# A two-layer trunk on one Trainium2 core: four reorderings in the projections and around the convolution output

## The chip, the cores and the metric

The kernel runs on one NeuronCore of a Trainium2 chip. The metric is the device time of one launch in microseconds; the number given for a kernel is the median of several runs. Besides that one execution is recorded by the hardware profiler, and all rows below come from it. The engines are PE (TensorE, matmuls), DVE (VectorE), ACT (ScalarE), POOL (GpSimd) and SP (SyncE, which here only issues DMAs). A DMA is issued by SP's or POOL's queue and runs beside the engines.

## The reference, cut to what matters

The trunk has two layers on a sequence of 1024 tokens with 1024 channels, all float32.

```python
# layer 0: gated short convolution
h = rms_norm(x, conv_norm)
b, c, u, z = split(h @ conv_w_in, 4)             # conv_w_in: 1024 x 8192
v = c * u
y = b * sum(conv_w[k] * shift(v, k)) * silu(z)   # causal, width 3
x1 = x + y @ conv_w_out                          # 2048 x 1024
# layer 1: dilated window attention, 3 groups x 16 heads of 64
h = rms_norm(x1, attn_norm)
qkv, z = split(h @ attn_w_in)                    # 3 groups x (q, k, v), and z
q, k = rms_norm(q, q_gain), rms_norm(k, k_gain)
o_g, lse_g = window_attention(q, k, v, rel_bias[t5_bucket])   # per group g
o = sum(softmax_g(lse_g) * o_g)
out = x1 + (o * silu(z)) @ attn_w_out
```

The row statistics of both norms (one factor per token) are applied after the products, since they commute with them.

## The kernel before

The work lies transposed: channels on the 128 partitions, tokens along the free axis, the tokens in two halves of 512 (`hf` 0 and 1). Every float32 operand of a product is split into a high part (ACT, line 169 for weights) and a low part (DVE, line 170), and a product is three matmuls: high with high, high with low, low with high. All matmuls of the projections are 128x128 with 512 columns.

There are four stages.

1. The convolution projections. 16 blocks `e` of 128 columns, four weights each (u, c, z, b). Blocks 0 and 1 are plain products (`products`, 24 matmuls each, lines 377 to 379). Blocks 2 to 15 go through `strassen`: two weights make a unit of seven products of 12 matmuls each (lines 304 to 307), on sums and differences of the four quadrants (T[1] to T[4] and the blocks B). Two units make one block e: in the first (`pr` = 0) u and c, in the second z and b. The seven products of a unit run in the order 1, 2, 4, 6, 5, 3, 7, where 4 and 3 are those of the unit before. `prepare` loads the two weights of the next unit meanwhile (SP, line 164, two raw tiles in all), forms four sums on POOL (line 279, the "mixes") and splits seven weights (eight "ws" tiles). A bank that more than one product adds to is first copied out by ACT (`copied`, line 312).
2. The convolution output: eight output tiles `dt` for each token half, 48 matmuls each (`chunk`, lines 554 to 556). `row` adds x, stores x1 to DRAM (line 565), and prepares the operands of the attention projections. In the second half it forms V1[i] and T[1] for dt = i under 4, and T[2] for dt = i + 4; both take the x1 of the first half back from DRAM (line 542).
3. The attention projections, again by `strassen`. T[3], T[4] and the lower block are made by `third`, `fourth` and `lower`, which are put between the products of the first two units. The product with T[3] is the last of the first unit.
4. The attention and its output product.

The row statistics of layer 0: `square` sums the squares of the x tiles on ACT and DVE into `sqacc`; `row_stats` takes the column sums by eight small matmuls for a half (line 94) into the one bank of the pool "cst", and DVE computes the reciprocal root in eleven small operations (lines 68 to 72); `row_spread` spreads it by four transposes (line 246) into that same bank, and ACT copies it to R and squares it to R2 (lines 247, 248). The evacuations `evac` of u, c and z need R or R2.

The tables of relative biases: `tables(v)` makes the bias of group v as one row per head (`vecd`, line 262), and `skew(v, h0)` writes it 128 times with a shift per copy, for four heads, into a DRAM table (line 268): a DMA on POOL's queue of 768 KB, or 512 KB for the third group. Twelve of them are traced, one at the start of the first unit of each block e from 4 to 15 (`between`). They are read in stage 4.

The order of the work: on PE the order of the program text holds everywhere. ACT is bound to it in the stretch from the first load to the end of block 0 (`manual_schedule`). Everywhere else, and on DVE, POOL and SP throughout stages 1 to 3, a planner orders the instructions when the kernel is built: it takes what is ready soonest by its own costs, so an instruction without open inputs can move ahead of others in the text. On each queue instructions then run strictly in the planned order. Tiles come from pools of fixed size; "f" has 12 tiles of 128x512, and a load into one waits for its last reader.

Of the kernel before, what the change touches and what calls it, by code (L numbers as in the profile page):

```python
# [19 lines left out]
P = 128  # L20
# [15 lines left out]
def trunk(ctx: ExitStack, tc: tile.TileContext, a, out):  # L36
# [103 lines left out]
    with tc.tile_pool(name="wq", bufs=1) as wq, tc.tile_pool(name="sle", bufs=1) as sle, \  # L140
# [32 lines left out]
        def load_x(hf):  # L173
            for kt in range(KT):
                xt = X[hf, kt] = ftile()
                if kt % 4 == 0:
                    B[kt // 4, hf] = block("abfg"[2 * hf + kt // 4])
                if hf == kt == 0:
                    r0 = raw_w(a["conv_w_in"][0, 0], 2)
                    W[0] = [split_w(r0[:, :HALF])]  # L180
                nc.sync.dma_start(xt, a["x"][hf, kt])
# [4 lines left out]
                if hf == kt == 0:  # L186
                    W[0].append(split_w(r0[:, HALF:]))
# [78 lines left out]
        def skew(v, h0):  # L266
            sk, w = ((sk0, 384), (sk1, 384), (sk2, 256))[v]
            nc.gpsimd.dma_start(sk[h0:h0 + 4].rearrange("h (i m) -> i h m", m=w + 1)[:, :, :w],
                                vecd[v, h0:h0 + 4][None, :, :w].to_broadcast([P, 4, w]))
# [68 lines left out]
        with tc.tile_pool(name="rp", bufs=1, side="right") as rp, tc.tile_pool(name="cp", bufs=2, side="right") as cp, \  # L338
# [62 lines left out]
            with tc.manual_schedule(engines={mybir.EngineType.Activation}):  # L401
# [15 lines left out]
                ps[1, 1] = products(1, 1, pp)  # L417
                row_spread(0)
                row_stats(1)
                ps[2, 1] = products(2, 1, pp)  # L420
                row_spread(1)
# [3 lines left out]
                ps[3, 0] = products(3, 0)  # L425
# [84 lines left out]
        with tc.tile_pool(name="ev", bufs=1, side="right", reuse_waits="tile") as ev, tc.tile_pool(name="xb", bufs=1, side="right", reuse_waits="tile") as xb, \  # L510
# [34 lines left out]
            B, T, V1 = {}, {}, {}  # L545
# [12 lines left out]
            def row(hf, dt):  # L558
# [19 lines left out]
                else:  # L578
# [4 lines left out]
                    parts_of(T[2], i, t)  # L583
                if dt == 0:
# [6 lines left out]
            def next_half(q):  # L591

                if q == 0:
                    load_y(1, 0)
                    for dt in range(2):
                        WO[dt, 0] = out_w(dt, 0)
                else:
                    load_y(1, q)

            load_y(0, 0)  # L600
            for dt in range(2):
# [3 lines left out]
            for hf in range(2):  # L605
                for dt in range(2):
                    WO[dt, 1] = out_w(dt, 1)
                for q in range(4):
                    for dt in range(2):
                        chunk(hf, dt, q)  # L610
                for dt in range(KT):
                    if dt > 1:
                        for c in range(2):
                            WO[dt, c] = out_w(dt, c)
                        if hf == 0 and dt == KT - 1:
                            next_half(0)
                        for q in range(4):
                            chunk(hf, dt, q)
                            if hf == 0 and dt == KT - 1 and q < 3:
                                next_half(q + 1)  # L620
                    row(hf, dt)
                    if hf == 1 and dt == 2:
                        stats(0, cst, sm)
                    elif hf == 1 and dt == 3:
                        spread(0, rtok, cst)
                    elif hf == 1 and dt == 4:
# [159 lines left out]
            def third(i):  # L786
                if i == 0:
                    T[3] = block("g")
                t = x1_tile(0, i)
                nc.vector.scalar_tensor_tensor(t, t, ng2[:, i:i + 1], V1[i], op0=OP.mult, op1=OP.add)  # L790
                parts_of(T[3], i, t)
# [451 lines left out]
```

## Time and profile before

| | |
|---|---|
| median of 3 runs | 2038.78 us (2037.06 to 2042.22) |
| profiled execution | 2040.09 us, its span 2038.1 us |
| PE busy | 1958.5 us, 96% |
| DVE, ACT, POOL busy | 1481.0 (73%), 903.5 (44%), 879.8 us (43%) |
| granted clock of PE, mean | 0.988 |
| moved by DMA | 254.25 MB, mean 125 GB/s |

How to read the rows below: times are in us from the span's start unless marked ns. In a row of the timeline the first number is the start, the second the length, then engine, line, operation, output and inputs; in brackets the idle time of the engine before it and what ended it. A matmul's length includes its way through the array, so the spacing of two starts is its cost. In rows of waits the engine and line that waited stand left of the arrow and what it waited for on the right. A granted clock of 1.00 is 2.4 GHz, 0.50 is 1.2 GHz.

### The profile page before, as it was taken

The numbers are of one execution on the slowest core, as the hardware profiler recorded it, in microseconds if no ns is written. First come the engines' busy times: TensorE is split into PE (matmuls) and PEld (weight loads), VectorE is DVE, ScalarE is ACT, GpSimd is POOL, SyncE is SP. The second block draws the span as 40 slices with busy tenths as digits, with TensorE's granted clock in tenths as the row PEclk, the third lists the DMA queues.
The fourth block names the chain that finished last, engine by engine and source line by source line (L and its number), as shares of the span: only waits on it lengthen the run. The fifth ranks groups of instructions, "written<-read, shape, count | busy, mean of one in ns | idle before, by whom it ended". The sixth has DMA issues, their size and how long they took to land. (4 is left out here: it accounts for less than half of the span.)

```text
span 2038.1 us, 29437 instructions
## 1 busy us (share of the span) xinstructions
PE 1958.5 (96%) x10302; PEld 1585.0 (78%) x10302; DVE 1481.0 (73%) x2751; ACT 903.5 (44%) x2042; POOL 879.8 (43%) x800
## 2 busy tenths in 40 slices
PE   7999999999999999999999999999999988898998
PEld 6887778888888888788888888888888866666666
DVE  6866566566666555798888888788888847767686
ACT  5433233333334344434344343444343358757570
POOL 0356566666665212434455445544445522322220
PEclk9999999999999999999999999999999999999999
DMA  5316512112214564423333233323233368766632
GB/s 189 114 62 146 141 61 73 68 67 73 72 64 152 178 228 159 131 76 111 102 105 123 84 111 97 123 83 121 86 124 104 91 241 248 219 175 207 181 115 84
DMA packets 116805, 254.25 MB, mean 125 GB/s; under 512 B 15822, under 2 KB 22718, under 8 KB 116656
## 3 DMA queue, kind: packets, MB, share of 16 engines
q1 hardware_dynamic: 93024, 177.42, 26.2%
q0 software_dynamic: 23632, 74.95, 12.9%
q8 instruction: 81, 1.33, 0.3%
q14 instruction: 68, 0.56, 0.1%
HBM read 193.05 MB, written 67.64 MB: 128 GB/s over the span
## 5 line engine op out<-in xcount | busy, mean ns | idle before, releaser
L170 DVE TENSOR_TENSOR ws<-wr,ws 128x512 fp32r<-128x512 f32 x284 | 270.2, 953 | 131.8 <-ACT ws L169 130.3
L169 ACT ACTIVATE ws<-wr 128x512 fp32r<-128x512 f32 x284 | 178.4, 630 | 395.6 <-PE pp L307 230.7
L169 ACT ACTIVATE ws<-sr 128x512 fp32r<-128x512 f32 x272 | 169.6, 629 | 295.9 <-PE pp L307 246.6
L279 POOL TENSOR_TENSOR sr<-wr 128x512 f32<-128x512 f32 x136 | 185.2, 1362 | 262.8 <-DMA wr<-in_conv_w_in 66.5
L170 DVE TENSOR_TENSOR ws<-sr,ws 128x512 fp32r<-128x512 f32 x272 | 235.6, 873 | 82.6 <-ACT ws L169 80.9
L898 ACT ACTIVATE xs<-xs,nl 128x128 f32<-128x128 f32 (+1 forms) x384 | 167.9, 439 | 91.2 <-DVE nl L895 80.2
L316 DVE TENSOR_TENSOR f<-pp,f 128x512 f32<-128x512 f32 x204 | 139.5, 684 | 85.5 <-PE pp L307 80.9
L895 DVE CUSTOM_DVE_ANT_0 xs<-ps,bt 128x128 f32<-128x128 f32 (+1 forms) x384 | 110.9, 347 | 79.5 <-PE ps L887 57.8
L312 ACT ACTIVATE f<-pp 128x512 f32<-128x512 f32 x228 | 132.5, 581 | 28.4 <-POOL blkc L683 13.4
L279 POOL TENSOR_TENSOR sr<-wr,sr 128x512 f32<-128x512 f32 x68 | 89.1, 1310 | 81.2 <-issue 57.6
L716 POOL DMA_DIRECT2D qkd<-blkc x96 | 68.1, 716 | 129.2 <-DVE blkc L711 121.8
L674 ACT ACTIVATE f<-f 128x512 f32<-128x512 f32 x96 | 60.7, 633 | 135.8 <-DVE f L316 98.8
L304 PE MATMUL pp<-blke,ws 128*128 128x512 f32 x272 | 108.7, 400 | 8.2 <-ACT f L312 8.2
L304 PE MATMUL pp<-blkg,ws 128*128 128x512 f32 x272 | 107.5, 395 | 4.8 <-ACT f L312 3.8
L306 PE MATMUL pp<-blkg,ws 128*128 128x512 f32 x272 | 106.7, 392 | 3.3 <-DVE blkg L524 3.3
L304 PE MATMUL pp<-blkf,ws 128*128 128x512 f32 x272 | 108.5, 399 | 0.7 <-ACT f L312 0.7
L304 PE MATMUL pp<-blka,ws 128*128 128x512 f32 x272 | 107.3, 395 | 0.7 <-ACT f L312 0.7
L306 PE MATMUL pp<-blke,ws 128*128 128x512 f32 x272 | 107.9, 397 | 0.0
L307 PE MATMUL pp<-blke,ws 128*128 128x512 f32 x272 | 107.8, 396 | 0.0
L304 PE MATMUL pp<-blkb,ws 128*128 128x512 f32 x272 | 107.4, 395 | 0.0
L304 PE MATMUL pp<-blkd,ws 128*128 128x512 f32 x272 | 107.0, 393 | 0.0
L887 PE MATMUL ps<-qk 64*128 64x128 f32 (+1 forms) x768 | 91.4, 355 | 15.7 <-DVE nl L895 8.6
(305 smaller groups left out, 5398.4 us busy)
## 6 DMA issues: line engine op xcount, KB each, us to landing
wr<-in_conv_w_in SPq DMA_DIRECT2D x128, 256.0 KB, 2.9
wr<-in_wqk SPq DMA_DIRECT2D x96, 256.0 KB, 3.0
qkd<-blkc POOLq DMA_DIRECT2D x96, 256.0 KB, 3.2
qk<-qkd SPq DMA_DIRECT2D x48, 512.0 KB, 7.1
wr<-in_conv_w_out SPq DMA_DIRECT2D x64, 256.0 KB, 3.2
f<-in_x SPq DMA_DIRECT2D x48, 256.0 KB, 4.5
wr<-in_wv SPq DMA_DIRECT2D x48, 256.0 KB, 2.9
vd<-f POOLq DMA_DIRECT2D x48, 256.0 KB, 2.4
```

What stands on the lines that cost most here:

```text
L169: nc.scalar.activation(t[:, 0], src, AF.Copy)
L170: nc.vector.tensor_tensor(t[:, 1], src, t[:, 0].bitcast(F32), op=OP.subtract)
L279: nc.gpsimd.tensor_tensor(t, x, y, op=op)
L304: nc.tensor.matmul(ps, w[:, 0, ws], b[:, k, 0], start=new and k == 0, stop=False, skip_group_check=not new)
L306: nc.tensor.matmul(ps, w[:, 0, ws], b[:, k, 1], start=False, stop=False, skip_group_check=not new)
L307: nc.tensor.matmul(ps, w[:, 1, ws], b[:, k, 0], start=False, stop=end and k == 3, skip_group_check=not new)
L312: nc.scalar.activation(t, ps, AF.Copy)
L316: nc.vector.tensor_tensor(m, ps, m, op=OP.add)
L716: nc.gpsimd.dma_start(qkd[hp, g, which].rearrange("p (c s) -> p c s", c=c) [:, :, hf * m:(hf + 1) * m], o.rearrange("p (c s) -> p c s", c=c))
L887: nc.tensor.matmul(out_, q[hs, b * P:(b + 1) * P], k[hs, kv], start=True, stop=True)
L895: nc.vector.tensor_tensor_reduce(out=x, in0=ps[s][:, x0:x0 + nk].rearrange("p a b -> p (a b)"), in1=u["bt"][s][:, bs], op0=OP.add, op1=OP. ...
L898: nc.scalar.activation(x, x, AF.Exp, bias=nm, scale=-1.0, accum_out=L)
```

## The change

Four edits; no arithmetic is added or left out.

1. `load_x`: the load of the first x tile is issued ahead of the two halves of the first weight (they were issued ahead of it). The split of the weight's first half follows the split of x tile 0, and that of its second half follows x tile 1.
2. `skew`: each of the twelve DMAs is bound behind the instruction that stands before it in the program text on POOL (`keep_in_program_order` sets an edge of issue order, without a wait for completion). From block 6 on that instruction is the last mix of the unit before.
3. Block 0: `row_spread(0)` and `row_stats(1)` move behind `products(2, 1)`, and `row_spread(1)` moves behind `products(3, 0)`; that product takes its bank from the pool "pp" and not from "cps".
4. The convolution output takes its tiles as 0, 4, 1, 5, 2, 6, 3, 7. For dt = i + 4 in the second half `row` now also loads the x1 tile i of the first half again and forms V3[i]; `third` only splits V3[i] into its two parts, where it loaded and formed it before. The places of `stats`, `spread` and `next_half` are counted by the position in the new order.

```diff
--- before.py
+++ after.py
@@ -175,15 +175,16 @@
                 xt = X[hf, kt] = ftile()
                 if kt % 4 == 0:
                     B[kt // 4, hf] = block("abfg"[2 * hf + kt // 4])
+                nc.sync.dma_start(xt, a["x"][hf, kt])
                 if hf == kt == 0:
                     r0 = raw_w(a["conv_w_in"][0, 0], 2)
-                    W[0] = [split_w(r0[:, :HALF])]
-                nc.sync.dma_start(xt, a["x"][hf, kt])
                 hi, lo = (B[kt // 4, hf][:, kt % 4, i] for i in range(2))
                 nc.scalar.activation(hi, xt, AF.Copy, scale=g1[:, kt:kt + 1])
                 nc.vector.scalar_tensor_tensor(lo, xt, g1[:, kt:kt + 1], hi.bitcast(F32), op0=OP.mult,
                                                op1=OP.subtract)
                 if hf == kt == 0:
+                    W[0] = [split_w(r0[:, :HALF])]
+                if hf == 0 and kt == 1:
                     W[0].append(split_w(r0[:, HALF:]))
                 if hf == 1:
                     square(0, kt)
@@ -265,8 +266,9 @@
 
         def skew(v, h0):
             sk, w = ((sk0, 384), (sk1, 384), (sk2, 256))[v]
-            nc.gpsimd.dma_start(sk[h0:h0 + 4].rearrange("h (i m) -> i h m", m=w + 1)[:, :, :w],
-                                vecd[v, h0:h0 + 4][None, :, :w].to_broadcast([P, 4, w]))
+            tc.keep_in_program_order(
+                nc.gpsimd.dma_start(sk[h0:h0 + 4].rearrange("h (i m) -> i h m", m=w + 1)[:, :, :w],
+                                    vecd[v, h0:h0 + 4][None, :, :w].to_broadcast([P, 4, w])))
 
         def prepare(s1_, s2_):
 
@@ -415,14 +417,14 @@
                     square(1, kt)
                 plain_w(0, 3, 2)
                 ps[1, 1] = products(1, 1, pp)
+                ps[2, 1] = products(2, 1, pp)
                 row_spread(0)
                 row_stats(1)
-                ps[2, 1] = products(2, 1, pp)
-                row_spread(1)
                 for k in range(3):
                     evac(0, k, 0, ps[k, 0])
                 next(mix)
-                ps[3, 0] = products(3, 0)
+                ps[3, 0] = products(3, 0, pp)
+                row_spread(1)
                 for k in range(3):
                     evac(0, k, 1, ps[k, 1])
                 evac(0, 3, 0, ps[3, 0])
@@ -542,7 +544,7 @@
                 nc.sync.dma_start(t, x1d[kt, :, half(hf)])
                 return t
 
-            B, T, V1 = {}, {}, {}
+            B, T, V1, V3 = {}, {}, {}, {}
             WO, ps = {}, {}
 
             def chunk(hf, dt, q):
@@ -581,6 +583,8 @@
                     t = V1[i]
                     nc.vector.scalar_tensor_tensor(t, x1, g2[:, dt:dt + 1], t, op0=OP.mult, op1=OP.subtract)
                     parts_of(T[2], i, t)
+                    t = V3[i] = x1_tile(0, i)
+                    nc.vector.scalar_tensor_tensor(t, t, ng2[:, i:i + 1], V1[i], op0=OP.mult, op1=OP.add)
                 if dt == 0:
                     nc.scalar.activation(sqacc[:, cs], x1, AF.Square)
                 else:
@@ -592,38 +596,39 @@
 
                 if q == 0:
                     load_y(1, 0)
-                    for dt in range(2):
+                    for dt in order[:2]:
                         WO[dt, 0] = out_w(dt, 0)
                 else:
                     load_y(1, q)
 
+            order = [0, 4, 1, 5, 2, 6, 3, 7]
             load_y(0, 0)
-            for dt in range(2):
+            for dt in order[:2]:
                 WO[dt, 0] = out_w(dt, 0)
             for q in range(1, 4):
                 load_y(0, q)
             for hf in range(2):
-                for dt in range(2):
+                for dt in order[:2]:
                     WO[dt, 1] = out_w(dt, 1)
                 for q in range(4):
-                    for dt in range(2):
+                    for dt in order[:2]:
                         chunk(hf, dt, q)
-                for dt in range(KT):
-                    if dt > 1:
+                for n, dt in enumerate(order):
+                    if n > 1:
                         for c in range(2):
                             WO[dt, c] = out_w(dt, c)
-                        if hf == 0 and dt == KT - 1:
+                        if hf == 0 and n == KT - 1:
                             next_half(0)
                         for q in range(4):
                             chunk(hf, dt, q)
-                            if hf == 0 and dt == KT - 1 and q < 3:
+                            if hf == 0 and n == KT - 1 and q < 3:
                                 next_half(q + 1)
                     row(hf, dt)
-                    if hf == 1 and dt == 2:
+                    if hf == 1 and n == 2:
                         stats(0, cst, sm)
-                    elif hf == 1 and dt == 3:
+                    elif hf == 1 and n == 3:
                         spread(0, rtok, cst)
-                    elif hf == 1 and dt == 4:
+                    elif hf == 1 and n == 4:
                         spread(0, ms2, cst)
 
 
@@ -786,9 +791,7 @@
             def third(i):
                 if i == 0:
                     T[3] = block("g")
-                t = x1_tile(0, i)
-                nc.vector.scalar_tensor_tensor(t, t, ng2[:, i:i + 1], V1[i], op0=OP.mult, op1=OP.add)
-                parts_of(T[3], i, t)
+                parts_of(T[3], i, V3[i])
 
             def fourth(i):
                 if i == 0:
```

## Rows read from the trace of the kernel before

**Rows 1.** Page, part 1: busy time, share of the span, instructions

```profile
PE 1958.5 (96%) x10302; PEld 1585.0 (78%) x10302; DVE 1481.0 (73%) x2751; ACT 903.5 (44%) x2042; POOL 879.8 (43%) x800
```

**Rows 2.** Windows of 100 us: each engine's busy time (matmuls), granted clock, DMA share

```profile
200.00:300.00 100.00, 92.19 (x384) 74.34 (x383) 60.06 (x64) 32.84 (x57) 58.46 (x50) 0.95 0.42 110
300.00:400.00 100.00, 100.00 (x443) 82.81 (x442) 66.14 (x75) 37.05 (x63) 64.19 (x50) 1.00 0.19 66
```

**Rows 3.** Waits of PE over the span: total, times, longest

```profile
PE pp L304 <- ACT f L312: 13.4, 15, 4.0
```

**Rows 4.** Timeline of POOL: start, length, operation [idle before, releaser]

```profile
193.15 3.02 POOL L268 DMA_DIRECT2D sk<-vecd  x4
214.95 1.28 POOL L279 TENSOR_TENSOR sr<-wr 128x512 f32<-128x512 f32 x1 [9.80 <-DMA wr<-in_conv_w_in]
```

**Rows 5.** DMA issues: count, KB each, median us from issue to landing

```profile
sk<-vecd POOLq DMA_DIRECT2D x8, 768.0 KB, 13.3
wr<-in_conv_w_in SPq DMA_DIRECT2D x128, 256.0 KB, 2.9
```

**Rows 6.** Line 475, once per pair of units; its timeline; PE's table products

```profile
L475 DVE TENSOR_TENSOR vb<-pp,f x14: 683/692/693, 128.7 to 640.6; 128x512 f32<-128x512 f32 x14
297.88 0.69 DVE L475 TENSOR_TENSOR vb<-pp,f 128x512 f32<-128x512 f32 x1 [0.34 <-PE pp L307]
L259 PE MATMUL st<-f,rel 33*16 33x512 f32 x6 | 3.1, 594 | 0.0
```

**Rows 7.** Timeline of ACT, then of PE, in a unit without skewed tables

```profile
282.18 0.58 ACT L312 ACTIVATE f<-pp 128x512 f32<-128x512 f32 x1
...
286.80 0.39 PE L304 MATMUL pp<-blke,ws 128*128 128x512 f32 x1
```

**Rows 8.** Timeline of DVE beside POOL's three mixes

```profile
190.02 3.77 DVE L170 TENSOR_TENSOR ws<-wr,ws 128x512 fp32r<-128x512 f32 x1
```

**Rows 9.** Timeline of PE around the row statistics, then ACT's copy, DVE

```profile
31.71 0.94 PE L94 MATMUL st<-ones,sqacc 128*128 128x1 f32 x8
37.87 0.39 PE L379 MATMUL pp<-blkg,ws 128*128 128x512 f32 x1
40.95 0.62 PE L246 MATMUL st<-ident,rt 128*128 128x128 f32 x4 [2.69 <-issue]
42.26 1.86 PE L94 MATMUL st<-ones,sqacc 128*128 128x1 f32 x8 [0.69 <-ACT R L247]
52.20 0.48 PE L377 MATMUL pp<-blka,ws 128*128 128x512 f32 x1
...
41.61 0.60 ACT L247 ACTIVATE R<-st 128x512 f32<-128x512 f32 x1 [1.51 <-PE st L246]
...
48.08 0.16 DVE L72 SCALAR_TENSOR_TENSOR rt<-rtt,rt 128x4 f32<-128x4 f32 x1
```

**Rows 10.** Timeline of PE at the start; ACT; landing of the eight x tiles

```profile
8.08 0.79 PE L377 MATMUL pp<-blka,ws 128*128 128x512 f32 x1 [8.08 <-ACT blka L183]
15.39 0.39 PE L377 MATMUL pp<-blka,ws 128*128 128x512 f32 x1
...
13.07 0.63 ACT L169 ACTIVATE ws<-wr 128x512 fp32r<-128x512 f32 x1 [0.23 <-DMA wr<-in_conv_w_in]
...
DMA to landing us min/median/max: 5.1/5.8/6.3
```

**Rows 11.** Timeline of PE behind the convolution output; then SP and DVE

```profile
844.86 0.39 PE L307 MATMUL pp<-blkd,ws 128*128 128x512 f32 x1
850.97 0.72 PE L306 MATMUL pp<-blkg,ws 128*128 128x512 f32 x1 [2.37 <-DVE blkg L524]
858.85 0.95 PE L94 MATMUL st<-ones,sqacc 128*128 128x1 f32 x8
...
831.29 19.36 SPq L542 DMA_DIRECT2D f<-x1d  x9
...
855.89 1.28 DVE L524 TENSOR_TENSOR blka<-f,blka 128x512 fp32r<-128x512 f32 x2
```

## The prediction

> **What bounds the kernel now.** I read the page first, then the windows, then the waits of PE and the timelines of the four stretches that the change touches. PE is busy 96% of the span [rows 1], and the windows show how: 100.00 of 100 us and 443 matmuls in a regular stretch of the convolution projections, but 92.19 us and 384 matmuls from 200 to 300 us, with a granted clock of 0.95 [rows 2]. So the time is the number of matmuls times their spacing, plus the places where PE stands still or runs at the lower of its two clock levels, 1.2 instead of 2.4 GHz. One regular pair of units is 168 matmuls and takes (640.6 - 297.88) / 9 = 38.08 us [rows 6], so 0.2267 us per matmul, 2.72 us per product of 12 and 5.44 us per plain product of 24. PE's order is written out by hand, so what a stretch loses or saves is carried to the end as it is. The longest group of waits is 13.4 us on ACT's copy of line 312 [rows 3]. The deficit of busy time from 200 to 300 us, 7.8 us [rows 2], is more than half as much, and leads to the skewed tables.
>
> **A, first x tile first.** Three transfers change places in SP's queue: x tile 0 goes ahead of the two halves of the first weight. No bytes are added. PE starts at 8.08, released by the high part of x tile 0; the second product starts at 15.39 [rows 10]. With x tile 0 first, PE can begin earlier, but x tiles 1 to 7 keep their places (they need 5.1 to 6.3 us from issue to landing), so only three matmuls of 24 really move. What is late next is the weight of the second product: its first half is on ACT at 13.07 for 0.63, that is 13.70 [rows 10], so the second product cannot move by more than 15.39 - 13.70 = 1.7 us. Below, nothing excludes 0, since ACT and DVE run the same operations on all eight x tiles. I take 0.8.
>
> **B, row statistics two products on.** Between the last matmul of the product before (37.87 + 0.23 = 38.10) and the start of products(3, 0) at 52.20 lie 14.10 us with only 24 matmuls in them [rows 9]. PE waits 2.69 us for the reciprocal root and 0.69 for ACT's copy out of the one "st" bank. The matmuls are 5.44 of the 14.10, the waits 3.38, the small products 0.35 twice and 0.94; the 3.6 us that are left are those in which PE runs at 1.2 GHz after the waits. I use these 3.6 us below as the price of a fall of the clock. After the change the 24 matmuls come first (43.54). The root of half 0 is long done by then (40.95). Four transposes take 0.35, and ACT's copy starts 0.66 after they do (40.95 to 41.61): copy from 44.2 to 44.8, the eight statistics matmuls 0.94 as at 31.71, products(3, 0) at 45.7 instead of 52.2. That is 6.5 us. The second spread, now behind products(3, 0), gives back 0.35 and must find the root of half 1 ready: it has 5.4 us, and in the trace it needed from 44.1 to 48.24 = 4.1 us [rows 9]. So 6.2 us. If that root is as slow as that of half 0 (32.65 to 40.95 = 8.3 us, DVE had splits in between), PE stands 2.9 us and pays 3.6 for the clock: 0.3 us is lost. Both ends are kept; I take 6.2, for the row of half 1 is the nearer one. The copy of R for half 1 now stands on ACT behind the three high parts of the first mix; what waits for it are DVE's evacuations of half 1, and their banks are wanted again two products later at the earliest, so I cost that at nothing; without that cover it would be the length of those ACT operations, some 2 us. products(3, 0) takes its bank from the other pool, whose third bank is free at that point.
>
> **C, skewed tables pinned.** Twelve DMAs on POOL's queue. Before, they leave in three groups of four, 3.02 us of issues each, at the first moment when their source row is there [rows 4]. The weight loads of the next unit then reach POOL's mix 9.80 us late [rows 4], since the four take 13.3 us to land against 2.9 for a weight load [rows 5]. Pinned, one leaves per pair of units, 38 us apart, always in the first unit of a pair. What the groups cost: from 128.7 to 297.88 four pairs took 169.2 us, four regular ones take 152.3; of the excess of 16.9 us the six table products are 3.1 [rows 6], which stay. 13.8 us can come back. What a lone one costs: a quarter of the group's transfer, 13.3 / 4 = 3.3 us, may stand before the loads. In a regular first unit ACT's copy of the bank ends at 282.76 and PE wants the bank again at 286.80 [rows 7], so 4.0 us of cover against 3.3: nothing to pay, but with 0.7 us to spare. Ends: 0 (each lone one costs its share of the old stalls, 13.8 / 12 = 1.15 us) and 13.8. I keep back 1.0 and take 12.8. On POOL's queue one issue of 0.76 is ahead of the mix; it was ahead of other mixes before.
>
> Here one more thing can be weighed. Beside POOL's three mixes a split of DVE took 3.77 us [rows 8], where an operation of that size takes 0.69 [rows 6]: 3.1 us more. The Trainium skill, page "SBUF — State Buffer", section "Who interferes with whom", has the rule behind it: a VectorE instruction with two SBUF inputs and a GpSimd instruction that reads SBUF exclude each other, and the one that comes second is blocked whole. The trace agrees on the mixes; for DMA issues no row shows it, as the four issues took 0.76 us each. If it held for a lone issue too, the cover would be short; that is a rival below.
>
> **D, output tiles as i and i + 4 in turn.** T[3] of the attention projections is now prepared in the rows of the second half (four loads and four DVE operations earlier, each of some 0.7 us, beside 10.88 us of matmuls per output tile), and only its two parts are left for the first unit. Without waits PE would go from 844.86 + 0.23 through 24 matmuls to the second statistics at 850.53; it got there at 858.85 [rows 11]. So 8.3 us stand to be won: waits for T[3], the longest 2.37 us, and the lower clock behind them. What is late next is T[4], wanted one product after the statistics, at 854.2, and finished at 857.17 in the trace [rows 11]. Four of the nine loads in SP's stretch of 19.36 us [rows 11] leave it, up to 8.6 us, and four DVE operations, some 3 us: T[4] comes at 848.6 to 854.2, in time at both ends, if narrowly. If it does not move, PE stands 3.0 us and pays 3.6 for the clock, and 8.3 - 6.6 = 1.7 us are left. I take 7.5. The other order of output tiles changes no count of matmuls, loads or stores.
>
> **Sum.** 0.8 + 6.2 + 12.8 + 7.5 = 27.3 us, with ends of 0 - 0.3 + 0 + 1.7 = 1.4 and 1.7 + 6.5 + 13.8 + 8.3 = 30.3. The profiled execution took 2040.09 (span 2038.1), 1.31 above the median of the runs: 2040.09 - 27.3 - 1.31 = 2011.5, say 2012 as the median.
>
> **Rivals.**
> 1. The pinned tables go on delaying weight loads, 1.15 us each, twelve times: C gives nothing, 2012 + 12.8 = 2025. For it: only 0.7 us to spare. Against: the loads of the pair's second unit, which stalled before, never meet one.
> 2. The exclusion of DVE and POOL holds for lone issues: 3.3 + 3.1 - 4.0 = 2.4 us of stall, twelve times 28.8, against the 13.8 that the groups cost: C loses 15.0, and the time is 2012 + 27.8 = 2040, no change. Against: the four issues of [rows 4]. By the Trainium skill, page "SBUF — State Buffer", section "Who interferes with whom", it would be so if the rule holds for the issue of a DMA as well.
> 3. T[4] or the loads behind it take the place of T[3]: D keeps 1.7 of 7.5, 2018. For it: the narrow 854.2. Against: the load and DVE time that leaves the stretch.
> 4. The change is slower. V1 and V3 hold eight of the twelve "f" tiles by the end of the second half, and SP issues in order: a load of V3 that finds no tile holds the output weights behind it. Such a stretch lasted 19.36 us [rows 11], while the weights reach one output tile ahead, 10.88 us; a stall is 8.5 us and 3.6 for the clock, 12.1. D's 7.5 go as well. From two such stalls on it is slower than before (2044), with three 2056. Against: by my count of what each row holds, ten or eleven tiles are taken at the worst.
> 5. DVE's, POOL's and SP's order is a planner's, and it plans anew around each edit; a new order may cost a few us anywhere: 2018 to 2045.
>
> **Chances.** Forecast 0.60, with its own range 2007 to 2016; rival 1 0.10; 2 0.05; 3 0.12; 4 0.06; 5 0.07. The range goes to rival 1 and over it a little, and below to a little under all gains in full: 2006 to 2027. Some 0.3%, 6 us, is what a measurement tells from no change. Faster: forecast, 1, 3 and half of 5, 0.86. Same: 2 and a little of 5, 0.07. Slower: 4 and a little of 5, 0.07.
>
> **What would show it.** A: PE's first matmul near 6, the second product near 14.5. B: no wait before the transposes of line 246, and products(3, 0) some 6 us nearer to the product before. C: twelve lone issues of line 268 some 38 us apart, the line-475 operations 38 to 39 us apart from the start, no PE wait on line 312 over 1 us between 140 and 300. D: T[3] complete before its product, 5.4 to 6 us from PE's last matmul with T[1] to the second statistics. The prediction is wrong if one of these stretches keeps its length, if a wait of PE on weights turns up in the output rows, or if the regular pair is longer than 38.08 us.

## The result, and the profile after

The changed kernel takes 2019.78 us in the median of six runs (2016.65 to 2024.06) against 2038.15 (2036.92 to 2042.22) before: a ratio of 0.9907, 95% interval 0.989 to 0.9923, so 16 to 22 us faster. The forecast was 2012 with a range of 2006 to 2027. The direction and that range held; the gain is 18.4 us where the sum had 27.3, and the forecast's own range, 2007 to 2016, did not hold.

First the page's busy times of the changed kernel, which answer to [rows 1]: the same 10302 matmuls, PE busy 11.4 us less and yet a larger share of a span of 2017.0 us.

```profile
PE 1947.1 (97%) x10302; PEld 1578.7 (78%) x10302; DVE 1487.5 (74%) x2751; ACT 904.0 (45%) x2042; POOL 883.9 (44%) x800
```

Two windows (busy time and matmuls of each engine, granted clock, DMA share). The stretch that had 92.19 us and 0.95 in [rows 2] is now full; its neighbour is as it was.

```profile
200.00:300.00 100.00, 100.00 (x440) 81.87 (x439) 66.55 (x76) 37.14 (x63) 66.42 (x53) 1.00 0.28 88
300.00:400.00 100.00, 100.00 (x443) 82.84 (x442) 65.06 (x71) 37.59 (x64) 70.14 (x54) 1.00 0.25 85
```

Since PE's order is fixed, the program can be cut at marks on its way and the pieces compared. The table has one profiled execution per kernel, the experiments below among them, in us: from the start to the first evacuation of a pair (line 475 before, 477 after), from it to the last, to the second row statistics of layer 1, from those to the transposes of rtok (the reciprocal root of the second norm, line 108), from the same statistics to the first turn of v (its transposes, line 727 or 732), to the first score product (887 or 890), to the last one, to the end, and the span.

```
                 start  pairs  output  to     stats    attn.  scores  rest   span
                               + T[3]  rtok   to turn  proj.
before           128.7  511.9  218.2   11.8   62.5     734.7  321.9   60.1   2038.1
before_again     128.2  510.4  217.3   11.8   62.6     734.4  325.2   60.0   2038.1
changed          123.0  498.6  210.1   14.7   67.0     736.3  323.5   58.5   2017.0
no_first_x       124.5  498.6  210.2   14.7   65.4     735.0  324.7   58.4   2016.8
no_stats_move    125.5  498.6  209.5   14.9   65.8     736.8  324.8   60.0   2021.0
no_pin           124.2  511.7  210.1   14.8   65.5     734.4  326.1   61.4   2033.4
no_order_no_v3   124.0  498.6  218.7   11.8   62.5     735.7  323.3   58.5   2021.3
root_later       123.0  498.6  210.2   17.7   62.3     735.3  325.9   61.5   2016.8
mix_behind_root  122.0  498.6  210.2   14.7   67.0     735.4  327.7   58.5   2019.4
table_early      123.1  498.6  210.2   14.8   65.6     736.9  325.6   58.4   2018.4
v3_late          125.1  498.6  217.1   11.8   62.5     734.9  327.4   58.4   2024.0
turn_undone      123.6  498.6  210.1   15.0   67.4     734.8  322.5   58.4   2015.4
root_and_table   123.3  498.6  210.4   17.7   62.2     735.9  325.7   58.4   2014.5
no_pool_mix      123.3  498.6  210.1   13.7   64.2     734.2  325.1   58.4   2013.9
```

The columns of the pairs, the output and rtok repeat within 1 to 1.5 us where the code is the same; the start scatters by 2.1 us in the seven with the same code there (changed, no_pin, no_order_no_v3, root_later, v3_late, turn_undone, no_pool_mix), the attention projections by 3, the scores by 6 and the rest by 3, whatever the kernel. So a term is read from its column, and a span or a median of few runs can't tell 2 us.

### The profile page after: what moved, and what is told of

Same layout as the page of the kernel before. It is cut to its first block, busy times and chain, and to the rows that moved or that the text cites. A ratio compares the mean times of both kernels' runs of the same rounds, so it can differ in the third digit from the quotient of the medians.

```text
span 2017.0 us, 29451 instructions
## 1 busy us (share of the span) xinstructions
PE 1947.1 (97%) x10302; PEld 1578.7 (78%) x10302; DVE 1487.5 (74%) x2751; ACT 904.0 (45%) x2042; POOL 883.9 (44%) x800
## 5 line engine op out<-in xcount | busy, mean ns | idle before, releaser
L170 DVE TENSOR_TENSOR ws<-wr,ws 128x512 fp32r<-128x512 f32 x284 | 276.1, 973 | 114.6 <-ACT ws L169 112.9
L170 DVE TENSOR_TENSOR ws<-sr,ws 128x512 fp32r<-128x512 f32 x272 | 228.0, 846 | 76.7 <-ACT ws L169 73.9
L314 ACT ACTIVATE f<-pp 128x512 f32<-128x512 f32 x228 | 132.5, 581 | 28.4 <-POOL blkc L688 14.6
L306 PE MATMUL pp<-blkg,ws 128*128 128x512 f32 x272 | 107.3, 394 | 4.4 <-ACT f L314 4.3
L306 PE MATMUL pp<-blkf,ws 128*128 128x512 f32 x272 | 108.5, 399 | 0.7 <-ACT f L314 0.7
L306 PE MATMUL pp<-blkb,ws 128*128 128x512 f32 x272 | 108.2, 398 | 0.0
L281 POOL TENSOR_TENSOR sr<-sr,wr 128x512 f32<-128x512 f32 x68 | 105.8, 1555 | 4.9
L309 PE MATMUL pp<-blkb,ws 128*128 128x512 f32 x272 | 106.8, 393 | 0.0
L308 PE MATMUL pp<-blkb,ws 128*128 128x512 f32 x272 | 106.5, 392 | 0.0
L309 PE MATMUL pp<-blkf,ws 128*128 128x512 f32 x272 | 106.4, 391 | 0.0
```

What stands on the lines that cost most here:

```text
L170: nc.vector.tensor_tensor(t[:, 1], src, t[:, 0].bitcast(F32), op=OP.subtract)
L281: nc.gpsimd.tensor_tensor(t, x, y, op=op)
L306: nc.tensor.matmul(ps, w[:, 0, ws], b[:, k, 0], start=new and k == 0, stop=False, skip_group_check=not new)
L308: nc.tensor.matmul(ps, w[:, 0, ws], b[:, k, 1], start=False, stop=False, skip_group_check=not new)
L309: nc.tensor.matmul(ps, w[:, 1, ws], b[:, k, 0], start=False, stop=end and k == 3, skip_group_check=not new)
L314: nc.scalar.activation(t, ps, AF.Copy)
```

## The experiments

All but one start from the changed kernel; times are medians beside runs of the kernel before on the same chip, and a mark "..." in a diff stands for lines left out.

**A taken back** (no_first_x).

```diff
-                nc.sync.dma_start(xt, a["x"][hf, kt])
                 if hf == kt == 0:
                     r0 = raw_w(a["conv_w_in"][0, 0], 2)
+                    W[0] = [split_w(r0[:, :HALF])]
+                nc.sync.dma_start(xt, a["x"][hf, kt])
...
                 if hf == kt == 0:
-                    W[0] = [split_w(r0[:, :HALF])]
-                if hf == 0 and kt == 1:
                     W[0].append(split_w(r0[:, HALF:]))
```

> Taken back from the changed kernel: the first weight group's transfer and splits ahead of the first x tile, as before. Theory that the parts add up: the second product starts at 15.4 instead of 14.2 us, everything behind it is later by the same 1.2 us, and the span is 2018.2 against 2017.0. Rival, that work behind hides the start: second product late by 1.2 us, but the spread of the second row half, which waits for a DVE chain and an x tile, starts at the same 51 us, and the span stays at 2017.0.

2019.48 us, ratio 0.9908 (0.9888 to 0.9929): no difference from the change as a whole. PE's first matmul comes at 7.51 instead of 6.63, its second product at 16.12. But that product scatters: 15.39 and 14.72 in the two executions before, 13.76 to 16.26 in the nine with x tile 0 first and ACT's table as it was. Nothing tells 1.2 us from 0 there; only the first matmul (6.97 to 8.08 without A, 6.58 to 6.75 with it) is clear.

**B taken back** (no_stats_move).

```diff
                 ps[1, 1] = products(1, 1, pp)
-                ps[2, 1] = products(2, 1, pp)
                 row_spread(0)
                 row_stats(1)
+                ps[2, 1] = products(2, 1, pp)
+                row_spread(1)
...
-                ps[3, 0] = products(3, 0, pp)
-                row_spread(1)
+                ps[3, 0] = products(3, 0)
```

> Taken back: the row statistics stand one product earlier again, as before. Theory of the prediction: both transposes wait for their roots and the lower clock follows, products(3,1) starts 6.2 us later than in the changed kernel and the span is 2023.2. Reading of the changed kernel's trace: of the 6.2 us only 4.6 had been won, since its DVE chain of the second root is held by the first mixing step's wait for an x tile; then products(3,1) starts 4.6 us later, near 56.6, and the span is 2021.6. Rival, that part of the gain came from elsewhere in the first 60 us: under 3 us.

2022.83 us, ratio 0.9932 (0.991 to 0.9953). products(3, 1) starts at 54.58 against 51.94 changed: 2.6 us, less than the two theories had and under the 3 us of the rival. 2.0 of the 2.6 are the later second product (16.26 against 14.22); from there on it is 38.3 us against 37.7, so that B is worth 0.6 us in this execution. By the ratios the runs give back 0.0025 of the time, 5 us, but the two intervals overlap, and the time decides nothing. The reason stands in two views, PE's timeline and windows of PE (busy time and matmuls, granted clock, DMA share). First the kernel with B taken back, then the second execution of the kernel before:

```profile
40.44 0.62 PE L247 MATMUL st<-ident,rt 128*128 128x128 f32 x4 [1.30 <-issue]
...
44.00:47.00 3.00, 3.00 (x15) 1.00 0.91 318
```

```profile
40.38 0.62 PE L246 MATMUL st<-ident,rt 128*128 128x128 f32 x4 [2.78 <-issue]
...
44.00:47.00 3.00, 3.00 (x9) 0.50 0.89 305
```

The transposes go at 40.4 in both, since they wait for the root. In the first, PE had begun its second product late (16.26) and waited 1.30 us, and the clock stayed at 2.4 GHz; in the second it waited 2.78 us and ran at 1.2 GHz in the whole window, as the first execution of the kernel before did (0.50 there too). By these executions, what B is worth depends on how early PE arrives: 4.7 us against the two of the kernel before (below), 0.6 against this one.

**C taken back** (no_pin: the pin alone; PE's, DVE's and SP's orders stay).

```diff
-            tc.keep_in_program_order(
-                nc.gpsimd.dma_start(sk[h0:h0 + 4].rearrange("h (i m) -> i h m", m=w + 1)[:, :, :w],
+            nc.gpsimd.dma_start(sk[h0:h0 + 4].rearrange("h (i m) -> i h m", m=w + 1)[:, :, :w],
```

> Taken back: the pin on the skewed tables alone; the order of PE, DVE and SP is that of the changed kernel, only POOL's and some of ACT's order differ. Theory of the prediction: four tables go out one behind the other on POOL again, PE waits some 13 us for the weights L312 there, and the span is 13.3 us longer, 2030.3. Rival, that the wait was opened by the earlier start and not by the tables' place: no wait above 1 us between 140 and 300 us, span within 1 us of 2017.0.

2030.56 us, ratio 0.9968 (0.9955 to 0.9982): by the ratios 0.0061 of the time, 12 us, is given back, and 13.1 us in the column of the pairs. Line 477 by source, POOL's timeline, PE's waits and the window, without the pin:

```profile
L477 DVE TENSOR_TENSOR vb<-pp,f x14: 684/692/693, 124.2 to 635.9; 128x512 f32<-128x512 f32 x14
...
189.64 3.02 POOL L269 DMA_DIRECT2D sk<-vecd  x4
212.06 1.26 POOL L281 TENSOR_TENSOR sr<-wr 128x512 f32<-128x512 f32 x1 [9.80 <-DMA wr<-in_conv_w_in]
...
PE pp L306 <- ACT f L314: 13.5, 15, 5.6
...
200.00:300.00 100.00, 91.52 (x384) 73.77 (x383) 59.43 (x65) 32.53 (x56) 59.77 (x50) 0.95 0.39 104
```

Every row of [rows 2 to 4] is back, with four issues in a row and the mix 9.80 us late. The rival, that the earlier start had done it, falls.

**D taken back** (no_order_no_v3: order = list(range(KT)), and V3 loaded and formed in third() as before).

> Taken back: the output tiles run 0 to 7 again and the third mixed operand's source is loaded and formed behind the last row, as before. The sum of the prediction: T[3] is late for its product again by some 6 us, and the span is 7.5 us longer, 2024.5. Reading of the changed kernel's trace: T[3]'s wait is back but the wait of 2.7 us for the second root, and the lower clock behind it, are gone, so it is longer by 3.6 us only, 2020.6. Rival, that the root was late for another reason (the start 13 us earlier of the whole stage): the root's wait stays and the span is over 2024.

2024.25 us, ratio 0.9933 (0.9917 to 0.9948). The output column is 8.6 us longer, the one from the statistics to the first turn 4.5 shorter than in the changed kernel's profile, the span 4.3 longer: T[3] is late and the root isn't. The reading of the trace holds.

**D's two halves.** First the early source undone and the turn of the tiles kept, then the other way round.

```diff
-                    t = V3[i] = x1_tile(0, i)
-                    nc.vector.scalar_tensor_tensor(t, t, ng2[:, i:i + 1], V1[i], op0=OP.mult, op1=OP.add)
             def third(i):
...
-                parts_of(T[3], i, V3[i])
+                t = x1_tile(0, i)
+                nc.vector.scalar_tensor_tensor(t, t, ng2[:, i:i + 1], V1[i], op0=OP.mult, op1=OP.add)
+                parts_of(T[3], i, t)
```

```diff
-            order = [0, 4, 1, 5, 2, 6, 3, 7]
+            order = list(range(KT))
```

> From the changed kernel: the output tiles stay i and i + 4 in turn, but the third mixed operand's source is loaded and formed behind the last row again. Theory that the early source is what brings T[3] in time: its waits of 5 to 6 us are back whole (L306, L308 on blkg near 830), the second statistics come 8 us later than in the changed kernel, the later root is no longer waited for, and the span is 2017.0 + 8 - 2.9, or 2022. Rival, that the turn of the tiles alone spreads DVE's work enough: waits on blkg under 2 us, span 2018 or less.

> From the changed kernel: the output tiles run 0 to 7 again, while the third mixed operand's source is still loaded and formed in the rows of tiles 4 to 7. Theory that the early source alone does it: no wait on blkg over 0.7 us, second statistics within 1 us of the changed kernel's, span within 1 us of 2017.0. Rival, that DVE has more to do in the last four rows than there is time for when they stand one behind the other (half 1's rows 4 to 7 each with two more operations): T[2], T[3] or the row's own add comes late and half or more of the 8 us returns, span 2020 or more.

v3_late: 2026.69 us, ratio 0.9951 (0.9933 to 0.9969). turn_undone: 2018.8 us, ratio 0.9907 (0.9893 to 0.9922), the changed kernel's. PE's timeline of each, from the waits for T[3] (blkg) on:

```profile
832.73 0.50 PE L308 MATMUL pp<-blkg,ws 128*128 128x512 f32 x1 [2.38 <-DVE blkg L526]
835.26 0.79 PE L308 MATMUL pp<-blkg,ws 128*128 128x512 f32 x1 [1.31 <-DVE blkg L526]
840.80 0.95 PE L94 MATMUL st<-ones,sqacc 128*128 128x1 f32 x8
852.63 0.60 PE L108 MATMUL st<-ident,rtok 128*128 128x128 f32 x4
```

```profile
832.35 0.95 PE L94 MATMUL st<-ones,sqacc 128*128 128x1 f32 x8
847.34 0.62 PE L108 MATMUL st<-ident,rtok 128*128 128x128 f32 x4 [3.00 <-DVE rtok L72]
```

Without the early source PE waits 3.7 us for T[3] (2.4 and 1.3, not the 5 to 6 expected), and the output column is 7.0 us longer. The early source alone brings T[3] in time; the turn of the output tiles, after which this part is named, adds nothing to it (210.1 us in both). Without the early source the turn may be worth a little: 217.1 us against 218.7 with both taken back, in one execution each, which is about the scatter.

**The root taken later** (root_later; ms2 are the mean squares under the root).

```diff
                 elif n == 1 and at == 4:
-                spread(1, rtok, cst)
+                spread(1, ms2, cst)
                 elif n == 1 and at == 6:
-                spread(1, ms2, cst)
+                spread(1, rtok, cst)
```

> On top of the changed kernel: in the second pair of attention projections the transposes of ms2 and of rtok change places, so that rtok's come two products later. Theory that the new wait of 2.7 us for the second row half's root (L108, rtok) is D's missing part: the wait goes, nothing is late next, the first L732 is 2.7 us earlier against the 896 to 898 us that the runs with the wait would have, and the span is 2014.3. Rival: DVE is the limit there (busy 27 of 30 us), the read of ms2's transposes stands behind the same DVE work, and rtok's transposes wait for their one PSUM buffer instead; the wait is 1.5 to 2.7 us at another place and the span stays within 1 us of 2017.0.

2017.28 us, ratio 0.9902 (0.9883 to 0.9921). The wait is gone and none takes its place: from the statistics to the first turn it is 62.3 us, as before the change (62.5), against 65.4 to 67.4 in the seven executions with the wait. rtok's transposes:

```profile
849.58 0.60 PE L108 MATMUL st<-ident,rtok 128*128 128x128 f32 x4
```

The span is 2016.8 all the same, because the scores and the rest took 5.4 us more in that execution, which is within the scatter of these columns.

**What made the root late** (no_pool_mix). Four POOL additions left out (plain is true for the third attention pair alone).

```diff
-                t = wq.tile([P, HALF], F32, name="sr", tag="sr", bufs=3)
-                nc.gpsimd.tensor_tensor(t, x, y, op=op)
+                t = x if plain else wq.tile([P, HALF], F32, name="sr", tag="sr", bufs=3)
+                plain or nc.gpsimd.tensor_tensor(t, x, y, op=op)
```

> On top of the changed kernel: the four POOL additions (L281) that mix the weights of the third attention pair are left out, and its products take unmixed weights (so the values of that pair of v are not the reference's); the order of PE, DVE, ACT and SP is the changed kernel's. In the changed kernel's trace three of these additions ran from 837.96 to 842.18 us, and in that time three DVE instructions took 1.81, 1.25 and 1.86 us that take 0.68, 0.17 and 0.74 elsewhere, 3.3 us more in front of the second root. Theory that POOL's additions stretch them: the three are short again, the root is ready 3.3 us earlier behind the statistics, L108's wait for rtok (2.7 us) is gone or under 0.3 us, and the span is some 2.5 us shorter. Rival, that the root is late by DVE's own queue alone (its first step starts 4.5 us behind the statistics): the three stay long or the chain waits elsewhere, and L108's wait is 2 us or more.

2016.86 us, ratio 0.9902 (0.9863 to 0.9941). Both theories hold half. First DVE's and POOL's timelines in the changed kernel:

```profile
836.18 0.14 DVE L100 TENSOR_SCALAR ms<-st 128x4 f32<-128x4 f32 x1
837.98 1.81 DVE L170 TENSOR_TENSOR ws<-wr,ws 128x512 fp32r<-128x512 f32 x1
839.71 1.25 DVE L70 TENSOR_TENSOR rtt<-rtok 128x4 f32<-128x4 f32 x1
840.88 1.86 DVE L529 SCALAR_TENSOR_TENSOR blkb<-f,attn_norm,blkb 128x512 fp32r<-128x512 f32 x1
846.10 0.11 DVE L72 SCALAR_TENSOR_TENSOR rtok<-rtt,rtok 128x4 f32<-128x4 f32 x1
...
837.96 1.28 POOL L281 TENSOR_TENSOR sr<-wr 128x512 f32<-128x512 f32 x1 [9.05 <-DMA wr<-in_wv]
839.32 1.61 POOL L281 TENSOR_TENSOR sr<-sr,wr 128x512 f32<-128x512 f32 x1
840.90 1.28 POOL L281 TENSOR_TENSOR sr<-wr 128x512 f32<-128x512 f32 x1
```

Then DVE's, ACT's and PE's without the additions:

```profile
838.29 0.68 DVE L170 TENSOR_TENSOR ws<-wr,ws 128x512 fp32r<-128x512 f32 x1
838.90 0.15 DVE L70 TENSOR_TENSOR rtt<-rtok 128x4 f32<-128x4 f32 x1
841.11 0.75 DVE L529 SCALAR_TENSOR_TENSOR blkb<-f,attn_norm,blkb 128x512 fp32r<-128x512 f32 x1 [2.06 <-ACT blkb L528]
...
840.35 0.72 ACT L528 ACTIVATE blkb<-f,attn_norm 128x512 fp32r<-128x512 f32 x1 [3.32 <-DMA f<-x1d]
...
845.70 0.62 PE L108 MATMUL st<-ident,rtok 128*128 128x128 f32 x4 [1.69 <-DVE rtok L72]
```

The three DVE instructions are short again, 1.13, 1.10 and 1.11 us less. But the third of them now waits 2.06 us for ACT, with the rest of the root's chain behind it in DVE's order, and PE's wait falls only from 2.68 to 1.69 us. ACT in its turn waited 3.32 us for a load of x1, a tile of B[1, 1]; it did so in the changed kernel too (3.30 us, ready at 840.74), where the stretched instructions covered it. So POOL's additions did stretch the chain, and that load, through DVE's order, held it besides; no run takes the load away.

The stretching is not what the change brought, though. With D taken back three instructions of the same chain are stretched as well (L71, L70 and L71 take 1.16, 1.15 and 1.23 us), and the root is in time: its first step comes 1.0 us behind the statistics (842.30 against 841.32) where it comes 4.5 us behind them in the changed kernel, and the chain takes 9.1 us against 10.0.

**B's missing part** (mix_behind_root). The first mixing step issued behind the second row spread.

```diff
-                next(mix)
                 ps[3, 0] = products(3, 0, pp)
                 row_spread(1)
+                next(mix)
```

> On top of the changed kernel: the first step of the mixed operands (loads of four x tiles, L218) is issued behind the second row spread instead of ahead of products(3,0). Theory that B's missing part is DVE's wait for the x tile inside the chain of the second root: L247's transposes no longer wait (1.18 us before), products(3,1) starts 1.2 us earlier relative to the second product, and the span is 2015.8. Rival, that the mixed operands are needed as early as they were: the first Strassen product that reads T[1] or T[2] waits, and the span is 2017 or more.

2021.05 us, ratio 0.9929 (0.9913 to 0.9945). This run doesn't tell: the planner kept the first subtraction (L218) inside the root's chain, where it waited 1.15 us for its x tile instead of 1.68, and PE's wait for the root fell from 1.18 to 0.65 us. That the chain without L218 would be in time wasn't shown by it; the next run says more.

**ACT's table** (table_early; warm is a new tile of one column).

```diff
+                nc.gpsimd.memset(warm, 0.0); nc.scalar.activation(warm, warm, AF.Copy)
                 load_x(0)
```

> On top of the changed kernel: a one-column activation stands ahead of the first x tile on ACT, so that the load of ACT's table (1.28 us) no longer begins when that tile lands. Theory that the table load is on the path: high part of x tile 0 at 4.1 instead of 5.3 us, first matmul at 5.4 to 5.7 instead of 6.6, second product 1 us earlier, span 2016.0. Rival, that the transfers set the first 16 us (16 engines busy 0.96 and 0.97 in 4:8 and 8:12): the first matmul is earlier, but the second product starts where the runs so far had it, 14.2 to 16.3 us, and the span does not move.

2017.58 us, ratio 0.9908 (0.989 to 0.9925). ACT's and PE's timelines, changed, then with the early table:

```profile
4.04 1.28 ACT L182 ACT_TABLE_LOAD   x1 [4.04 <-DMA f<-in_x]
5.34 0.72 ACT L182 ACTIVATE blka<-f,conv_norm 128x512 fp32r<-128x512 f32 x1
...
6.63 0.79 PE L379 MATMUL pp<-blka,ws 128*128 128x512 f32 x1 [6.63 <-ACT ws L169]
```

```profile
0.74 1.28 ACT L405 ACT_TABLE_LOAD   x1 [0.74 <-PEq L1238]
4.10 0.72 ACT L182 ACTIVATE blka<-f,conv_norm 128x512 fp32r<-128x512 f32 x1 [1.86 <-DMA f<-in_x]
...
5.49 0.80 PE L379 MATMUL pp<-blka,ws 128*128 128x512 f32 x1 [5.49 <-ACT ws L169]
8.56 0.80 PE L379 MATMUL pp<-blka,ws 128*128 128x512 f32 x1 [1.42 <-ACT blka L182]
```

The first matmul is 1.1 us earlier, but PE then waits 1.42 us at the fourth, whose x tile isn't there (ACT waited 2.35 us for it), and the second product starts at 15.40, as the rival had it: the transfers set the pace.

This profile also bears on B's missing part. DVE's and PE's timelines with the early table:

```profile
50.56 0.69 DVE L218 TENSOR_TENSOR f<-f 128x512 f32<-128x512 f32 x1 [0.59 <-DMA f<-in_x]
...
51.66 0.62 PE L247 MATMUL st<-ident,rt 128*128 128x128 f32 x4
```

The statistics of half 1 came 1.2 us later here than in the changed kernel (44.92 against 43.74), and L218's x tile at nearly the same time. So DVE waited 0.59 us for it instead of 1.68, and PE did not wait for the root at all; from the second product to products(3, 1) it is 36.6 us instead of 37.7. It is one profile, but it has the missing 1.2 us go with the wait for the x tile.

**The kernel before once more** (before_again).

> The kernel before once more, for the scatter of stages that the change does not touch. If the second half of the program differs by scatter alone, the stretch from the first score product L887 to the last (321.9 us in the first execution) comes out anywhere between 321 and 326, as the five runs behind the change did with 323.3 to 326.1, and the start may or may not show the lower clock behind the transposes L246. If the change costs that stage 2 to 3 us, it is 321.9 again within 0.5 us.

2040.07 us in its one run. The scores took 325.2 us instead of 321.9, so that no cost of the change shows there; and the start has the wait and the lower clock again.

**Both mends** (root_and_table).

> Both on top of the changed kernel: rtok's transposes two products later, and ACT's table loaded ahead of the first x tile. The first took its wait of 2.7 us away (time 2017.28), the second made the first matmul 1.1 us earlier and the second product no earlier in its one profile. Theory that only the root is worth something: 2017. Rival, that the table's 1.28 us count too where transfers come well: 2016 or less.

2016.31 us (five runs), ratio 0.9893 (0.9879 to 0.9908): the best of all by its median. Its interval overlaps that of the change, 0.989 to 0.9923, so that only the column of the statistics (62.2) shows a gain, by the root; the start column (123.3) shows none by the table.

## Why the prediction came out as it did

**A** was sized 0.8. PE starts 0.85 us earlier in the mean (7.52 over three executions to 6.67 over nine), and the second product hardly moves. The step overlooked that ACT's table load, hidden at 0.74 us before, would move behind the wait for x tile 0; but putting it back helped the first matmul alone, so what holds the second product is the transfers.

**B** was sized 6.2. From the second product to products(3, 1) it was 42.4 and 42.5 us in the two executions before and is 37.7: 4.7. The step that failed is that the root of half 1, which "needed from 44.1 to 48.24 = 4.1 us", would be ready in the 5.4 us that it has. It took 6.6 (44.79 to 51.42), 2.5 more: 0.8 because two evacuations still stand in front of its first step on DVE (L239), 1.0 because L71 took 1.14 us beside a POOL multiplication (L354, 46.50 us), and 0.8 because L218, which had its place in the chain before too (as L217), waited 1.68 us for its x tile instead of 0.91. PE's transposes, DVE's chain:

```profile
51.56 0.62 PE L247 MATMUL st<-ident,rt 128*128 128x128 f32 x4 [1.18 <-DVE rt L72]
...
45.59 0.15 DVE L239 TENSOR_SCALAR ms<-st 128x4 f32<-128x4 f32 x1
46.65 1.14 DVE L71 SCALAR_TENSOR_TENSOR rtt<-rtt,ms 128x4 f32<-128x4 f32 x1
50.45 0.69 DVE L218 TENSOR_TENSOR f<-f 128x512 f32<-128x512 f32 x1 [1.68 <-DMA f<-in_x]
51.26 0.16 DVE L72 SCALAR_TENSOR_TENSOR rt<-rtt,rt 128x4 f32<-128x4 f32 x1
```

Both together, by the start column, gave 5.0 us (128.5 to 123.5 in the mean of the ten executions with both, 123.7 in the seven without another edit there) where 7.0 stood. That is measured against two executions of the kernel before; B taken back alone gave less in its one execution, as said.

**C** was sized 12.8 and is 12.5 (511.2 to 498.6). Twelve lone issues, and the pair at its regular length; line 477, the issues and their landing by source, and the longest of PE's waits on L314, against [rows 3 to 6]:

```profile
L477 DVE TENSOR_TENSOR vb<-pp,f x14: 691/692/693, 123.0 to 621.6; 128x512 f32<-128x512 f32 x14
...
L270 POOL DMA_DIRECT2D sk<-vecd x12: 777/782/806, 173.5 to 592.9; - x12
DMA to landing us min/median/max: 5.7/6.8/7.5
...
PE pp L306 <- ACT f L314: 5.7, 12, 1.3
```

A lone table lands in 6.8 us, not 3.3 as the quarter had it. POOL's mix behind eleven of the twelve lone tables waits 1.6 to 5.3 us for its weight, 2.3 in the median, against 1.1 to 1.5 in the units between and 6.4 to 9.8 behind the groups. So the load is late by about a microsecond, and the cover holds, though not by the sum that was made for it: PE does not wait between 140 and 300 us, and from 120 to 640 us once for line 314, 0.7 us. 13 pairs at 38.08 and the 3.1 of the table products make 498.1 of the 498.6. Rivals 1 and 2 fall.

**D** was sized 7.5. T[3] came in time and brought 7.6 (217.8 to 210.1 us), T[4] is not waited for, and no output weight was late: rivals 3 and 4 fall as they were put. What failed is "what is late next": that was the root of the second half, behind the very statistics that now came earlier. Before, its last step was at 869.38 and its transposes at 870.66, 1.3 us to spare, and no row of the prediction asked for it. Now its first step on DVE (L100) comes 4.5 us behind the statistics instead of 1.5 (860.38 against 858.85), since T[4] and B[1, 1] are still being formed there, and its chain takes 10.0 us instead of 9.1. DVE's and PE's timelines before, then PE's after, from the last matmul with T[1]:

```profile
860.38 0.15 DVE L100 TENSOR_SCALAR ms<-st 128x4 f32<-128x4 f32 x1
869.38 0.15 DVE L72 SCALAR_TENSOR_TENSOR rtok<-rtt,rtok 128x4 f32<-128x4 f32 x1
...
870.66 0.60 PE L108 MATMUL st<-ident,rtok 128*128 128x128 f32 x4
```

```profile
826.01 0.39 PE L309 MATMUL pp<-blkd,ws 128*128 128x512 f32 x1
...
831.68 0.95 PE L94 MATMUL st<-ones,sqacc 128*128 128x1 f32 x8
846.36 0.62 PE L108 MATMUL st<-ident,rtok 128*128 128x128 f32 x4 [2.68 <-DVE rtok L72]
```

5.67 us to the statistics, as foretold; then 14.7 to the transposes instead of 11.8. By the column from the statistics to the first turn the wait costs 2.9 to 3.3 us, and 4.5 to 4.9 where the clock fell behind it, so that a fall costs some 1.6 us there where the prediction took 3.6. D keeps 3 to 5 of its 7.5.

**The sum.** 5.0 + 12.5 + 7.6 less a mean of 3.7 for the root is 21.4 us of the 27.3; B's root and D's root make nearly all of the rest. That the median shows 18.4 lies within its interval; the columns behind the first turn, where the change does nothing, scatter by more than the difference. The range of 2006 to 2027 held because it reached past the forecast's own 2016, to rival 1: A, B and D all gave less than they were sized at, and only C came out at its size. Rival 3's 2018 is near the time, but T[4] was not late; the root cut D, and a load behind T[4]'s had its part in that.

## What to carry to other kernels

When a wait is taken off a fixed order, look for the next value that the order will want, and compare how long its chain takes with the time that it then has; here each such chain ran on an engine whose queue held other work inside it. Read small terms from marks in the trace, not from spans whose later stages scatter by 6 us. Take a change apart into its edits: the edit after which a part is named may be the one that does nothing.

## What the hardware showed beside this

- DVE instructions on 128x4 elements took 1.14 and 1.25 us instead of 0.16 beside a POOL operation on two SBUF tiles, and 0.15 without it. That is the rule of the Trainium skill, page "SBUF — State Buffer", section "Who interferes with whom" (of a VectorE instruction with two SBUF inputs and a GpSimd instruction that reads SBUF, the one that comes second is blocked whole), and this trace agrees: L71 ended at 47.79, the POOL operation beside it at 47.78; for the lone DMA issues on POOL it was not seen, as they took 0.78 us, and a split of DVE beside the first of them 0.69 (at 173.84).
- Behind PE's wait for the root the granted clock differs between executions of the same instructions, windows of PE and the others, in the changed kernel and then with A taken back:

```profile
847.00:850.00 3.00, 3.00 (x9) 2.34 (x9) 0.41 (x1) 0.60 (x1) 1.27 (x1) 0.54 0.03 10
```

```profile
847.00:850.00 3.00, 1.99 (x11) 1.76 (x12) 2.15 (x6) 2.02 (x4) 0.72 (x1) 1.00 0.00 0
```

It was at 1.2 GHz for some 3 us in three of the seven executions with a wait of 2.7 to 3.0 us there, and not in the one with 1.7 us.
